# First retention outputs loaded and split during the last pair of gate columns of a streaming encoder layer

## The chip, the cores and the metric

One core of a Trainium2 chip. The metric is the device time of one execution in microseconds; the time before is the median of three runs. The profile is of one further execution. The engines: PE (TensorE, matmuls), DVE (VectorE), ACT (ScalarE), POOL (GpSimd) and SP (SyncE, which here only issues DMAs). Each engine takes its instructions in the order in which the program holds them.

## The reference

One step of a hybrid encoder layer over 1024 prompt tokens and 64 sample tokens, width 1024, all in float32:

```
rq, rk, rv, rg, sq, sk, sv, ga, gb = split(rms_norm(x) @ w_in)
A = (rms_norm(retention(rq, rk, rv)) * silu(rg)) @ w_ret_out     # 4 heads of 256
B = sliding_window_attention(sq, sk, sv, bias, sinks) @ w_swa_out  # 16 heads of 64
x += (sigmoid(ga) * A + sigmoid(gb) * B) @ w_mix_out
x += cross_attention(rms_norm(x), memory)                        # 256 memory tokens
x += swiglu(rms_norm(x))
y = rms_norm(x)
```

The sliding window takes chunks of 64 queries against their own and the two earlier chunks (192 keys). States, keys, values and memory keys and values are outputs too.

## The kernel before

Activations lie transposed: 8 tiles of 128 features by 1088 tokens. Float32 precision is made from two float32r parts: an operand is **split** into a high part (a cast on ACT, L123) and a low part (a subtraction on DVE, L124), and each product is three matmuls (high x high, high x low, low x high). `load` (L117) and `store` (L120) issue DMAs from SP. Weights come as 128x1024 pieces into two staging buffers `raw` and are split into `wq` tiles.

**The projections** run as pairs of column blocks. A pair is seven block products of a Strassen-like scheme (`strassen`, L205 to L208), in the order of the operands B11, B21, T2, T1, T3, B22, T4. Each product fills an accumulator of two PSUM banks (three such accumulators), which DVE adds up (L252, L563) and scales (L569); for gate columns ACT takes the sigmoid (L572) and issues the store (L658). The last pair of all is the last of `w_gb`.

**The places.** Two rings of eight SBUF places each hold the operands, two places an operand (ring 0: B11 in 4 and 5, T1 in 6 and 7, T4 in 0 and 1, the stage tiles for outputs in 2 and 3; ring 1: B21 in 0 and 1, T2 in 4 and 5, T3 in 6 and 7, B22 in 2 and 3). A later tile in a place waits until the last reader of the earlier one is through, so the places come free in the order of the products.

**The passage to attention** (`mix_phase`). Two streams of work are interleaved on PE. The sliding-window attention (`swa`) goes through 34 halves of chunks: scores `pss` (L934), softmax (DVE L944 or L947 with the bias, L949 to L954, ACT L956 and L958, DVE L959 and L960, POOL L962), transposes `pp` (L976), their copies `pT` (ACT L979, DVE L981), weighted values `pout` (L992). A `filler` puts other products between them: the last of the memory values (`pd<-wq,ms`), then the retention outputs times `w_ret_out` (`pd<-ret,wq`), with half an output block (12 matmuls) after each half chunk. `filler` first loads all retention outputs from the scratch tensor `d_gate[0]` in three groups of columns (384, 384, 320, eight loads each), through ten small tiles `lds`, and splits them into the eight `ret` tiles of ring 1; then come the weights, one unit `w_ret_out[m]` at a time.

**What sets the order.** A scheduler orders the instructions of each engine at build time; `tc.high_priority()` moves work up, `tc.issue_after(x)` places work behind instruction x in its order (it adds no wait on the chip). The order on PE of the passage is written out with `in_order`. The eight tiles `flat[0..7]` of ring 0 (places 4, 5, 6, 7, 0, 1, 2, 3) hold what attention reads: keys `kT` (flat[0], place 4, with three token tiles), queries `qTs` (flat[1] and flat[7]), bias (flat[2], place 6), token values `vT` (flat[5], place 1), transposed tokens `vts` (flat[4], place 0), and `lds` (flat[3] and flat[6], places 7 and 2).

Of the kernel before, what the change touches and what calls it, by code (L numbers as in the profile page):

```python
# [2 lines left out]

# [1 line left out]

# [14 lines left out]
P = 128  # L20
D = 1024
KT = D // P
# [3 lines left out]
CH = ((0, 384), (384, 384), (768, 320))  # L26
# [9 lines left out]
NPAIR = 8  # L36
NKEY = 192
KC = SEQ + P + SMP
# [71 lines left out]
class Kernel:  # L110
# [760 lines left out]
    def swa(self, ctx, fill):  # L871
        nc, tc, io = self.nc, self.tc, self.io
        if True:
# [2 lines left out]
            mm = nc.tensor.matmul  # L876

            flat = [t.rearrange("p a b -> p (a b)") for t in self.ring_tiles(0, KT, "swin", F32)]
            kT, vT = flat[0][:, :KC], flat[5][:, :KC]
            bias = flat[2][:, :NPAIR * NKEY].rearrange("p (a b) -> p a b", b=NKEY)  # L880
            sinks = self.sinks
            qTs = [t[:, :16 * 2 * 64].rearrange("p (i c e) -> p i c e", i=4, c=4) for t in (flat[1], flat[7])]
            vts = [flat[4][:, i * P:(i + 1) * P] for i in range(17)] + [flat[0][:, KC + i * P:KC + (i + 1) * P] for i in range(3)]
            self.lds = [t[:, i * 384:(i + 1) * 384] for t in (flat[3], flat[6]) for i in range(5)]
            with tc.high_priority():
                def tokens(dst, i, cache):
                    self.load(dst[:, :SEQ], self.d_skv[i, :, :SEQ])
                    self.load(dst[:, SEQ:SEQ + P], io[cache])
                    self.load(dst[:, SEQ + P:], self.d_skv[i, :, SEQ:])
# [5 lines left out]
            with tc.high_priority(), tc.issue_after(self.loaded):  # L895
                for e in range(2):
                    src = self.d_rb.rearrange("(p e) c -> e c p", e=2)[e, 63:63 + 64 * 255, :]
                    src = src.rearrange("(i c) p -> i p c", c=255)[:, :, :NKEY]
                    self.load(bias[e * 64:(e + 1) * 64], src)
            def keep():  # L900
                for src, o in ((kT, "o_sk"), (vT, "o_sv")):
                    self.store(io[o][0], src[:, SEQ - P:SEQ])
                    self.store(io[o][1], src[:, SEQ + SMP:KC])
# [21 lines left out]

            def scores(c, hf):
                ks, j0, nk = keys(c)
                if hf == 0 and c % 4 == 0 and c + 4 < 17:
                    self.load_queries(qTs, c + 4)
                qT = qTs[c // 4 % 2]  # L930
                pss = pw.tile([P, 2, 512], F32, tag="s", name="pss")
                for i in range(2):
                    for v in range(2):
                        self.last_mm = mm(pss[:, v, i * NKEY:i * NKEY + nk], qT[rows[v], 2 * hf + i, c % 4, :],  # L934
                                          kT[rows[v], ks:ks + nk], start=True, stop=True).ins
                quad = lambda x: x.rearrange("p (v h i) -> p v h i", v=2, h=2)[:, :, hf, :]
                snk = quad(sinks)
                t = sw.tile([P, 2, 2, NKEY], F32, tag="t", name="t")
                ps = pss[:, :, :2 * NKEY].rearrange("p v (i n) -> p v i n", n=NKEY)
                bs = bias.rearrange("p (v h i) n -> p v h i n", v=2, h=2)  # L940
                nm = sw.tile([P, 2, 2], F32, tag="nm", name="nm")
                if nk == NKEY:
                    fl = lambda x: x.rearrange("p v i n -> p v (i n)")
                    nc.vector.scalar_tensor_tensor(fl(t), pss[:, :, :2 * NKEY], 0.125, fl(bs[:, :, hf]), ALU.mult, ALU.add)  # L944
                else:
                    for v in range(2):
                        nc.vector.scalar_tensor_tensor(t[:, v, :, :nk], ps[:, v, :, :nk], 0.125, bs[:, v, hf, :, j0:],  # L947
                                                       ALU.mult, ALU.add)
                nc.vector.tensor_reduce(nm, t[:, :, :, :nk], AX.X, ALU.max)  # L949
                nc.vector.tensor_tensor(out=nm, in0=nm, in1=snk, op=ALU.max)  # L950
                nc.vector.tensor_scalar(nm, nm, -1.0, None, ALU.mult)
                den = sw.tile([P, 2, 2], F32, tag="den", name="den")
                es = sw.tile([P, 2, 2], F32, tag="es", name="es")
                nc.vector.tensor_tensor(out=es, in0=snk, in1=nm, op=ALU.add)  # L954
                for v, i in units:
                    nc.scalar.activation(t[:, v, i, :nk], t[:, v, i, :nk], AF.Exp, bias=nm[:, v, i:i + 1],  # L956
                                         accum_out=den[:, v, i:i + 1])
                nc.scalar.activation(es, es, AF.Exp)  # L958
                nc.vector.tensor_tensor(out=den, in0=den, in1=es, op=ALU.add)  # L959
                nc.vector.reciprocal(den, den)  # L960
                p = lambda x: x.rearrange("p v i n -> p (v i) n")
                nc.gpsimd.tensor_tensor(out=p(t)[:, :, :nk], in0=p(t)[:, :, :nk], op=ALU.mult,  # L962
                                        in1=den.rearrange("p v i -> p (v i)").unsqueeze(2).broadcast_to([P, 4, nk]))
                live[c, hf] = t
# [41 lines left out]
            n = len(halves)  # L1006
            for i in range(-2, n):
                if i > 0:
                    self.in_order(lambda: weigh(*halves[i - 1]))
                if i + 2 < n:  # L1010
                    self.in_order(lambda: scores(*halves[i + 2]))
                if i >= 0:
                    self.in_order(lambda: turn(*halves[i]))
                for pieces in next(fill):
                    self.in_order(lambda: next(pieces, None))
                if i == -2:
                    with tc.high_priority(), tc.issue_after(self.operand_loaded):
                        tokens(vT, 1, "cvT")
                if i == 8:
                    with tc.issue_after(self.loaded):  # L1020
                        keep()
# [23 lines left out]
    def filler(self):  # L1045

        nc, tc, io = self.nc, self.tc, self.io
        if True:
            def ld():
                self.lds.append(self.lds.pop(0))  # L1050
                return self.lds[-1]

            rets = self.ring_tiles(1, KT, "ret")

            def operands(c0, n):
                after = self.loaded
                for k in range(KT):
                    a = ld()
                    with tc.issue_after(after):
                        ins = self.load(a[:, :n], self.d_gate[0][k, :, c0:c0 + n])  # L1060
                    if c0 == 0:
                        self.operand_loaded = ins
                    self.split(a[:, :n], rets[k][:, 0, c0:c0 + n], rets[k][:, 1, c0:c0 + n])

            for c0, n in CH:
                operands(c0, n)
            us, h = self.first_units, H - 1
            for t in range(2):
                ps = self.dense_psum()
                for k in range(KT):  # L1070
                    x = self.ms[k][:, :, t * P:(t + 1) * P]
                    self.mm3(ps[:, :256], x[:, 0], x[:, 1], *us[k // 4][k % 4], k == 0, k == KT - 1)
                    if k == 3:
                        yield
                o = ld()[:, :256]
                with tc.high_priority():
                    nc.scalar.mul(o, ps[:, :256], self.mtok[:, t:t + 1])
                self.store(self.d_mv[h, :, t, :], o)
                self.store(io["o_mv"][t * P:(t + 1) * P, h * 256:(h + 1) * 256], o)
                yield  # L1080
            for m in range(KT):
                u = self.unit(io["w_ret_out"][m], KT)
                for c0, n in CH:
                    g = ld()
                    self.load(g[:, :n], self.d_gate[1][m, :, c0:c0 + n])
                    for ps in self.pieces(u, rets, c0, n):
                        if ps is None:
                            yield
                    nc.vector.tensor_tensor(out=g[:, :n], in0=ps, in1=g[:, :n], op=ALU.mult)
                    self.store(self.d_mix[m, :, c0:c0 + n], g[:, :n])  # L1090
                    yield
# [588 lines left out]
```

## Time and profile before

| | |
|---|---|
| median of 3 runs | 2251.56 us (2247.32 to 2252.81) |
| the profiled execution | 2246.01 us |
| its span, first to last instruction | 2244.2 us |
| mean granted clock of TensorE | 0.988 |
| last pair of gate columns, first matmul | 793.1 us after the span's start |
| first scores of the attention | 814.1 us |
| first product with retention outputs | 835.1 us |
| last scores of the attention | 1002 us |

Rows of a timeline give the start in us from the span's start, the duration, the engine, the line of the kernel, the operation with output <- input tiles, the size, and in brackets the idle time of the engine before it and what ended it. A row with xN has N instructions merged. Rows of a table of stretches give the length, the busy time of PE, PEld (weight loads), DVE, ACT and POOL with their instructions, the granted clock of TensorE, the busy share of the DMA engines and GB/s. DMA rows give the size of one transfer and the median time from issue to landing.

### The profile page before, as it was taken

How to read it: one execution, taken by the hardware profiler on the slowest of the kernel's cores; microseconds unless marked ns; L12 is line 12 of the kernel's file. 1: busy time of each engine (PE TensorE's matmuls, PEld its weight loads, DVE VectorE, ACT ScalarE, POOL GpSimd, SP SyncE). 2: the span in 40 equal slices, each digit the busy share in tenths (PEclk: the TensorE clock that was granted, in tenths of full speed). 3: DMA queues.
4: the chain of work that ended last, by engine and by line, in shares of the span. 5: the costliest groups of instructions: out<-in, count | busy, mean ns of one | idle time of the engine just before them, and what ended most of it. 6: DMA issues, size and time to landing. Idle time of an engine off the chain costs nothing.

```text
span 2244.2 us, 41644 instructions
## 1 busy us (share of the span) xinstructions
PE 2161.9 (96%) x16374; PEld 2097.0 (93%) x16374; DVE 1602.8 (71%) x2655; ACT 883.9 (39%) x1896; POOL 689.8 (31%) x466
## 2 busy tenths in 40 slices
PE   7899999999999989999999999999999999999996
PEld 6899999999999977779999998999999999999986
DVE  8995878676687568875455565676777777778587
ACT  7333333435444355553233343333222222344343
POOL 1441533342263112220000000015555556434462
PEclk9999999999999989999999999999999999999998
DMA  5433345443545475327343112422342332476233
GB/s 198 161 116 110 111 130 134 130 127 115 172 141 188 144 242 166 111 68 219 118 153 119 38 49 71 133 78 88 122 138 92 102 128 83 151 263 196 75 96 108
DMA packets 182598, 290.84 MB, mean 130 GB/s; under 512 B 40290, under 2 KB 110850, under 8 KB 182402
## 3 DMA queue, kind: packets, MB, share of 16 engines
q1 hardware_dynamic: 177794, 279.26, 39.2%
q10 hardware_dynamic: 4608, 8.91, 1.1%
q8 instruction: 129, 2.11, 0.4%
q14 instruction: 67, 0.55, 0.1%
HBM read 196.95 MB, written 91.16 MB: 128 GB/s over the span
## 4 chain that ended last, share of the span: by engine, by line
PE 80%; DVE 10%; DMA 4%; issue 2%; ACT 2%; POOL 1%; SPq 0%; DVEq 0%; ACTq 0%; POOLq 0%
PE pq L208 15%; PE pq L205 15%; PE pq L206 15%; PE pd L149 8%; PE pd L151 8%; PE pd L150 8%; DVE wq L124 2%; PE pout L992 1%; DMA hl<-d_op 1%; PE pp L976 1%; PE pss L934 1%; DVE T L124 1%; DVE B L124 1%; DMA qs<-d_qkv 1%; PE pk L691 1%
## 5 line engine op out<-in xcount | busy, mean ns | idle before, releaser
L124 DVE TENSOR_TENSOR wq<-raw,wq 128x512 fp32r<-128x512 f32 (+1 forms) x505 | 456.6, 908 | 126.4 <-ACT wq L123 124.2
L123 ACT CAST wq<-raw 128x512 fp32r<-128x512 f32 (+1 forms) x505 | 307.7, 614 | 562.6 <-PE pq L208 266.5
L205 PE MATMUL pq<-T,wq 128*128 128x272 f32 x1832 | 492.5, 289 | 5.6 <-DVE u L252 3.7
L206 PE MATMUL pq<-T,wq 128*128 128x272 f32 x1832 | 492.8, 289 | 0.0
L206 PE MATMUL pq<-B,wq 128*128 128x272 f32 x1592 | 430.1, 290 | 9.7 <-DVE B L124 9.5
L205 PE MATMUL pq<-B,wq 128*128 128x272 f32 x1592 | 428.0, 289 | 11.8 <-ACT wq L123 10.6
L208 PE MATMUL pq<-T,wq 128*128 128x272 f32 x1832 | 384.1, 290 | 3.6 <-DVE wq L124 3.6
L183 POOL TENSOR_TENSOR raw<-raw 128x512 f32<-128x512 f32 (+1 forms) x59 | 82.7, 1402 | 905.9 <-DVE wq L124 623.6
L205 PEld LDWEIGHTS pq<-T,wq 128*128 128x128 f32 x1832 | 346.0, 189 | 6.3 <-DVE u L252 3.7
L206 PEld LDWEIGHTS pq<-T,wq 128*128 128x128 f32 x1832 | 346.0, 189 | 0.3 <-issue 0.3
L208 PE MATMUL pq<-B,wq 128*128 128x272 f32 x1592 | 334.2, 290 | 0.0
L206 PEld LDWEIGHTS pq<-B,wq 128*128 128x128 f32 x1592 | 301.2, 189 | 12.2 <-DVE B L124 11.8
L205 PEld LDWEIGHTS pq<-B,wq 128*128 128x128 f32 x1592 | 300.8, 189 | 12.5 <-ACT wq L123 10.6
L208 PEld LDWEIGHTS pq<-T,wq 128*128 128x128 f32 x1832 | 291.0, 190 | 5.1 <-DVE wq L124 4.4
L208 PEld LDWEIGHTS pq<-B,wq 128*128 128x128 f32 x1592 | 253.5, 190 | 0.5 <-issue 0.3
L252 DVE TENSOR_TENSOR u<-pq,u 128x544 f32<-128x544 f32 x177 | 127.5, 721 | 112.3 <-PE pq L208 111.7
L186 POOL TENSOR_TENSOR raw<-raw 128x512 f32<-128x512 f32 (+1 forms) x59 | 83.1, 1408 | 133.8 <-DVE wq L124 126.2
L563 DVE TENSOR_TENSOR stage<-pq,u 128x544 f32<-128x544 f32 x112 | 80.3, 717 | 27.7 <-PE pq L208 25.3
L962 POOL TENSOR_TENSOR t<-t,den 128x768 f32<-128x768 f32 (+2 forms) x34 | 47.9, 1407 | 167.4 <-DVE nm L950 58.7
L184 POOL TENSOR_TENSOR raw<-raw 128x512 f32<-128x512 f32 (+1 forms) x59 | 88.1, 1494 | 3.7
L189 POOL TENSOR_TENSOR raw<-raw 128x512 f32<-128x512 f32 (+1 forms) x59 | 84.0, 1424 | 4.4
L1438 POOL TENSOR_TENSOR y<-u,y 128x544 f32<-128x544 f32 x38 | 61.9, 1638 | 76.3 <-DVE y L1436 52.0
(370 smaller groups left out, 4647.2 us busy)
## 6 DMA issues: line engine op xcount, KB each, us to landing
hl<-d_op SPq DMA_DIRECT2D x85, 272.0 KB, 4.0
d_qkv<-stage SPq DMA_DIRECT2D x44, 272.0 KB, 2.1
d_op<-stage SPq DMA_DIRECT2D x44, 272.0 KB, 2.1
d_op<-ht SPq DMA_DIRECT2D x44, 272.0 KB, 3.2
raw<-w_gate SPq DMA_DIRECT2D x22, 512.0 KB, 3.4
raw<-w_up SPq DMA_DIRECT2D x22, 512.0 KB, 3.6
d_gate<-stage ACTq DMA_DIRECT2D x32, 272.0 KB, 2.3
raw<-w_down SPq DMA_DIRECT2D x16, 512.0 KB, 4.4
```

What stands on the lines that cost most here:

```text
L123: self.last_cast = self.nc.scalar.copy(hi, src).ins
L124: return self.nc.vector.tensor_tensor(out=lo, in0=src, in1=hi.bitcast(F32), op=ALU.subtract).ins
L149: mm(ps, wh, xh, start=start, stop=False)
L150: mm(ps, wh, xl, start=False, stop=False)
L151: self.last_mm = mm(ps, wl, xh, start=False, stop=stop).ins
L184: tt(out=a21, in0=a21, in1=a22, op=add)
L186: tt(out=a11, in0=a22, in1=a11, op=sub)
L189: tt(out=a12, in0=a12, in1=a11, op=sub)
L205: mm(ps[:, c, :HC], w[:, 0, ks], x[:, 0, cs], start=start, stop=False)
L206: mm(ps[:, c, :HC], w[:, 0, ks], x[:, 1, cs], start=False, stop=False)
L208: self.last_mm = mm(ps[:, c, :HC], w[:, 1, ks], x[:, 0, c * HC:(c + 1) * HC], start=False, stop=stop).ins
L252: add = lambda out, a, b: nc.vector.tensor_tensor(out=out, in0=a, in1=b, op=ALU.add)
```

## The change

The eight `ret` tiles get their places of ring 1 in the order in which the last pair frees them (0, 1, 4, 5, 6, 7, 2, 3). The loads and splits of the first 384 columns are free to be scheduled from the moment when the first places come free; they go through five `lds` tiles in B11's first place (flat[0]), the other five (flat[5], T4's second place) join afterwards. The attention's tiles move: keys and the three token tiles to flat[2], bias to flat[3] (T1's places), values to flat[4] (T4's first place), transposed tokens to flat[6] (a stage place); the queries stay. `w_ret_out[0]` is loaded and split ahead of the other two groups of columns, which come behind the bias's load in the order; the load of the value tokens comes behind the bias too. The second load of queries (chunks 4 to 7), issued before with the first scores, comes behind the last load of retention outputs.

```diff
-            kT, vT = flat[0][:, :KC], flat[5][:, :KC]
-            bias = flat[2][:, :NPAIR * NKEY].rearrange("p (a b) -> p a b", b=NKEY)
+            kT, vT = flat[2][:, :KC], flat[4][:, :KC]
+            bias = flat[3][:, :NPAIR * NKEY].rearrange("p (a b) -> p a b", b=NKEY)
...
-            vts = [flat[4][:, i * P:(i + 1) * P] for i in range(17)] + [flat[0][:, KC + i * P:KC + (i + 1) * P] for i in range(3)]
-            self.lds = [t[:, i * 384:(i + 1) * 384] for t in (flat[3], flat[6]) for i in range(5)]
+            vts = [flat[6][:, i * P:(i + 1) * P] for i in range(17)] + [flat[2][:, KC + i * P:KC + (i + 1) * P] for i in range(3)]
+            self.lds, self.more_lds = ([t[:, i * 384:(i + 1) * 384] for i in range(5)] for t in (flat[0], flat[5]))
...
-                    self.load(bias[e * 64:(e + 1) * 64], src)
+                    self.bias_loaded = self.load(bias[e * 64:(e + 1) * 64], src)
...
-                if hf == 0 and c % 4 == 0 and c + 4 < 17:
+                if hf == 0 and c % 4 == 0 and 0 < c < 13:
                     self.load_queries(qTs, c + 4)
...
                 if i == -2:
-                    with tc.high_priority(), tc.issue_after(self.operand_loaded):
+                    with tc.high_priority(), tc.issue_after(self.bias_loaded):
                         tokens(vT, 1, "cvT")
+                    with tc.issue_after(self.last_operand):
+                        self.load_queries(qTs, 4)
...
-            rets = self.ring_tiles(1, KT, "ret")
+            rets = [self.rings[1].tile(f"ret{k}", slot=i) for k, i in enumerate((0, 1, 4, 5, 6, 7, 2, 3))]
 
             def operands(c0, n):
-                after = self.loaded
+                after = self.bias_loaded
                 for k in range(KT):
                     a = ld()
-                    with tc.issue_after(after):
-                        ins = self.load(a[:, :n], self.d_gate[0][k, :, c0:c0 + n])
-                    if c0 == 0:
-                        self.operand_loaded = ins
+                    with tc.issue_after(after) if c0 else nullcontext():
+                        self.last_operand = self.load(a[:, :n], self.d_gate[0][k, :, c0:c0 + n])
                     self.split(a[:, :n], rets[k][:, 0, c0:c0 + n], rets[k][:, 1, c0:c0 + n])
-
-            for c0, n in CH:
+                if c0 == 0:
+                    self.lds += self.more_lds
+
+            operands(*CH[0])
+            first = self.unit(io["w_ret_out"][0], KT)
+            for c0, n in CH[1:]:
                 operands(c0, n)
...
-                u = self.unit(io["w_ret_out"][m], KT)
+                u = self.unit(io["w_ret_out"][m], KT) if m else first
```

More of the change, by code (lines that the diff above doesn't have):

```diff
@@ L1 @@
 import math
-from contextlib import ExitStack, contextmanager
+from contextlib import ExitStack, contextmanager, nullcontext
 import numpy as np
```

## The prediction

> **What bounds the kernel now.** I read the engine shares and the chain of work on the page first, then the stretch where the change acts: where TensorE waits between 790 and 860 us, and what each queue does there.
>
> ```profile
> PE 2161.9 (96%) x16374; PEld 2097.0 (93%) x16374; DVE 1602.8 (71%) x2655; ACT 883.9 (39%) x1896; POOL 689.8 (31%) x466
> PE 80%; DVE 10%; DMA 4%; issue 2%; ACT 2%; POOL 1%; SPq 0%; DVEq 0%; ACTq 0%; POOLq 0%
> ```
>
> TensorE (PE) bounds the whole: 2161.9 of 2244.2 us. Only its 82 us of idle time, and matmuls at a low clock, can be won. The waits of PE from 790 to 1010 us (total, times, longest):
>
> ```profile
> PE pd L149 <- ACT wq L123: 7.9, 2, 5.2
> PE pp L976 <- POOL t L962: 1.2, 2, 0.8
> PE pout L992 <- ACT pT L979: 1.2, 1, 1.2
> ```
>
> Nearly all of it is the passage from the gate columns to the sliding-window attention (SWA). PE's timeline there (start, us, idle before and releaser in brackets):
>
> ```profile
> 817.55 0.58 PE L149 MATMUL pd<-wq,ms 128*128 128x256 f32 x1 [2.78 <-ACT wq L123]
> 823.31 0.28 PE L149 MATMUL pd<-wq,ms 128*128 128x256 f32 x1
> 826.24 0.66 PE L934 MATMUL pss<-swin,swin 64*128 64x64 f32 x8
> 829.65 0.33 PE L911 MATMUL pd<-ident,swin 128*128 128x128 f32 x1 [0.80 <-DMA swin<-d_skv]
> 835.14 0.69 PE L149 MATMUL pd<-ret,wq 128*128 128x384 f32 x1 [5.16 <-ACT wq L123]
> 841.50 0.63 PE L976 MATMUL pp<-ident,t 128*64 128x128 f32 x4
> 841.88 0.42 PE L149 MATMUL pd<-ret,wq 128*128 128x384 f32 x1
> 845.57 0.66 PE L976 MATMUL pp<-ident,t 128*128 128x128 f32 x4
> 845.98 0.42 PE L149 MATMUL pd<-ret,wq 128*128 128x384 f32 x1
> 849.52 0.65 PE L992 MATMUL pout<-pT,swin 128*64 128x256 f32 x4 [1.21 <-ACT pT L979]
> 851.88 0.66 PE L976 MATMUL pp<-ident,t 128*128 128x128 f32 x4 [0.85 <-POOL t L962]
> 856.15 1.04 PE L976 MATMUL pp<-ident,t 128*128 128x128 f32 x8
> ```
>
> There are two holes, 2.78 us before the last memory-value product and 5.16 us before the first retention output product, and after each the clock is low:
>
> ```profile
> 815.00:820.00 5.00, 2.31 (x9) 2.02 (x10) 3.17 (x6) 3.78 (x8) 0.00 (x0) 0.64 0.71 240
> 830.00:835.00 5.00, 0.00 (x0) 0.00 (x0) 3.50 (x12) 5.00 (x21) 1.71 (x2) 0.51 0.91 320
> 835.00:840.00 5.00, 4.24 (x12) 3.56 (x12) 5.00 (x10) 3.75 (x10) 0.23 (x1) 0.50 0.97 310
> ```
>
> (Busy time of PE, PEld, DVE, ACT, POOL, then granted clock, DMA share, GB/s.) After the first hole the slow pace lasts from 817.55 to 823.31, 5.8 us. After the second, the same three steps (12 matmuls, pout, scores) take 835.14 to 841.50, 6.36 us with 0.62 of waiting in it, and 841.88 to 845.57, 3.69 us, one step later: the low clock costs 5.74 - 3.69 = 2.05 us. Both holes end with a cast of ACT:
>
> ```profile
> 815.73 0.66 ACT L572 ACTIVATE stage<-stage 128x544 f32<-128x544 f32 x1 [2.33 <-DVE stage L569]
> 816.88 2.18 ACT L123 CAST wq<-raw 128x512 fp32r<-128x512 f32 x4 [0.49 <-ACT stage L572]
> 834.48 2.18 ACT L123 CAST wq<-raw 128x512 fp32r<-128x512 f32 x4
> ```
>
> **The change part by part.** The built program holds the same instructions: 24 loads and 24 splits of retention outputs (a cast on ACT, a subtraction on DVE), the same matmuls. What changes is where they stand.
>
> *Splits of the first 384 columns* (8 of 24) stand inside the last pair. Row durations of all splits:
>
> ```profile
> 838.45 2.40 DVE L124 TENSOR_TENSOR ret<-swin,ret 128x384 fp32r<-128x384 f32 x5
> 841.07 1.70 DVE L124 TENSOR_TENSOR ret<-swin,ret 128x320 fp32r<-128x320 f32 x4 [0.23 <-ACT ret L123]
> 836.55 1.70 ACT L123 CAST ret<-swin 128x384 fp32r<-128x384 f32 x4
> 794.79 0.32 SPq L117 DMA_DIRECT2D swin<-d_skv  x1
> 793.10 0.29 PE L205 MATMUL pq<-B,wq 128*128 128x272 f32 x1
> 814.11 0.66 PE L934 MATMUL pss<-swin,swin 64*128 64x64 f32 x8
> 794.00:814.00 20.00, 20.00 (x163) 19.96 (x161) 9.38 (x13) 4.88 (x8) 1.94 (x2) 1.00 0.78 227
> ```
>
> One costs 0.48 us of DVE (0.43 for 320 columns) and 0.43 of ACT. Eight add 3.8 to DVE's 9.38 and 3.4 to ACT's 4.88 of 20 us, beside a PE that is busy throughout. The pair's seven products run from 793.10 to 814.11, 3.0 us each; half through the first, at 794.79, the first place came free for a load. Each split waits for the product that frees its place (B21, T2, T3, B22, in this order), as the add standing next to it does, and three accumulators lie between an add and the product that needs its bank: I cost this at 0. Were the cover gone, the dearest place is one 0.5 us subtraction ahead of an add. The lower bound is 0 too.
>
> *The first hole stays.* ACT casts the w_mv pieces behind the last sigmoid (815.73), which hangs on the last product. Their loads now stand behind eight gate loads (192 KB each), the queries (1 MB) and the keys (0.6 MB) on SP. With their own 1 MB that is 4.2 MB; at the 227 GB/s of the last row it takes 18.5 us from 794.8, to 813, and the cast comes at 816.88. 0 us.
>
> *w_ret_out ahead of the other columns; values' load moved up.* The value tokens load when T4's first place is free (half through the last product, 812.6), so the 0.80 at 829.65 goes. The w_ret_out load waits for a staging buffer, freed by the second w_mv subtraction:
>
> ```profile
> 817.52 2.50 DVE L124 TENSOR_TENSOR wq<-raw,wq 128x512 fp32r<-128x512 f32 x4 [1.82 <-ACT wq L123]
> 829.62 0.81 SPq L117 DMA_DIRECT2D raw<-w_ret_out  x2
> raw<-w_ret_out SPq DMA_DIRECT2D x5, 512.0 KB, 5.9
> ```
>
> That is 818.8 instead of 829.62; SP holds six loads of the second 384 columns, all of the last 320, and two more units behind it. With the median of 5.9 us it lands at 824.7, its cast ends by 826, before PE needs it. So the first product of retention outputs no longer waits 5.16 and 0.62: PE gets there at 829.0 (826.24, two score steps, token transpose, pp), does its 12 matmuls at full pace and comes to the next pp at 832.3.
>
> *What is late next.* That pp (841.50 before) transposes the second softmax tile. Before, it was long ready:
>
> ```profile
> 830.83 0.61 POOL L962 TENSOR_TENSOR t<-t,den 128x256 f32<-128x256 f32 x1 [5.19 <-DVE nm L951]
> 829.54 0.68 DVE L949 TENSOR_REDUCE nm<-t 128x4 f32<-128x512 f32 x1
> 842.69 0.75 DVE L947 SCALAR_TENSOR_TENSOR t<-pss,swin 128x256 f32<-128x256 f32 x2
> ```
>
> In the changed order DVE has, between this tile's scores (which PE gives at 826.9) and its reciprocal (L960, on which POOL's scaling waits): 5 subtractions of 384 columns (2.4), 8 of 320 (3.4), 4 of w_ret_out (2.5), three score evacuations L947 (0.5, 0.75, 0.75), three maxima L949 (0.4, 0.7, 0.7), and about twelve small ones of 0.09 (1.1): 13.2 us. ACT likewise has the tile's last exponential behind the last cast. DVE is through at 840.1, POOL's 0.61 ends at 840.8, and PE stands from 832.3 to 840.8, 8.5 us. **The wait changes its place**: pp starts at 840.8 instead of 841.50.
>
> *After it*, the low clock comes again: pp 0.4, three steps in 5.74 (as after 835.14), pp 0.4, then four steps as from 841.88 to 845.98 (3.7): the next pp at about 851.0 (before 851.88), the one after, 4.27 later, at 855.2 (before 856.15). The 1.21 and 0.85 of waiting are gone, paid for by the slow steps that now come later. POOL scales the next two tiles right behind the first (by some 844, an estimate from the same rows), before PE asks for them. From 860 on PE waited for SWA only once,
>
> ```profile
> PE pp L976 <- POOL t L962: 0.4, 1, 0.4
> ```
>
> so nothing gives it back, and nothing more is won.
>
> **Sum:** 856.15 to 855.2, -1.0 us. On the profiled execution (2246.0, span 2244.2 and 1.8 around it) that is 2245.0; this execution lies 5.6 below the median 2251.56, so I put 2250.6 for the median.
>
> The Trainium skill, "TensorE: Matmul & The Clock Gate", Part 1, says that the gate closes after an idle window of about 3.4 us and that sustained work opens it again after about 3.4 us. The trace differs: the pace fell after only 2.78 us of idle and stayed low for 5.8 us. With the page's 3.4 us the steps after 840.8 would be done some 0.7 us sooner, an estimate from that page, and the sum -1.7.
>
> **The rivals.**
>
> *The holes go for good.* If DVE's list is through by 832, PE never stands: pp at 832.3 instead of 841.50 (-9.2), and the 1.21 and 0.85 go as well: about -10, 2241.5. For it: the cause of the longest wait is truly removed. Against: DVE's 13.2 us would have to fit in 5.4, and its order is fixed in the program; it decides only if those rows take less than half.
>
> *The transfers bind, and it gets slower.* From 818.8 until the last of the 24 loads, SP brings 3 x 512, 6 x 192, 8 x 160 and 4 x 64 KB: 4.3 MB, behind a load that waits for DVE.
>
> ```profile
> 819.00:847.00 28.00, 20.74 (x129) 17.61 (x128) 22.94 (x59) 20.41 (x64) 2.72 (x3) 0.74 0.93 305
> 805.00:810.00 5.00, 5.00 (x42) 5.00 (x41) 2.45 (x4) 0.00 (x0) 0.00 (x0) 1.00 1.00 206
> d_qkv<-stage SPq DMA_DIRECT2D x44, 272.0 KB, 2.1
> ```
>
> At 305 GB/s, with 2 us from issue to landing, they are in by 835, some 4 us before DVE wants the last; at the 206 of the other stretch, by 842: pp at 844 (+2.5), and the gate columns and units behind it late by as much again: +5, 2256. Below some 250 GB/s this decides. Against it: the bytes before 819 are fewer than those that moved at 305.
>
> *It does not do what it says*: the early loads come too late to split under the last pair. They are issued from 794.8, when B11's first place is free; at 227 GB/s the first five with the 1 MB of queries take 9 us, and the fifth place frees at 807: no.
>
> **How the numbers follow.** Wait moved: 0.65, from -4 to +2.5 (3 us of ACT and DVE order either way, and the executions before lay at 2247.3 to 2252.8). Holes gone: 0.15. Transfers bind: 0.15, half of it beyond 0.3%. None of these: 0.05. 0.3% is 6.8 us, about what a measurement of this kernel tells from no change. Faster 0.17, same 0.72, slower 0.11. The range leaves out the holes-gone case: 2243 to 2256.
>
> **What would show it.** Right: no wait before the first pd<-ret; a hole of 7 to 9 us before the second pp, released by POOL; 2.78 us before pd<-wq,ms unchanged; low clock near 845. Wrong: POOL's second scaling before 835, or PE waiting for a load of the gate columns, or for an add inside the last pair.

## The result, and the profile after

The changed kernel takes **2257.97 us** (median of 7 runs, 2257.38 to 2261.46), the kernel before on the same chip 2250.23 (7 runs, 2246.79 to 2255.4): ratio **1.0041**, 95% interval 1.0031 to 1.005. It is slower, by 7.7 us in the medians and 9 by the ratio, and above my range (2243 to 2256).

The shares of the page (busy time, then the chain that ended last) look as before:

```profile
PE 2167.4 (96%) x16374; PEld 2104.4 (93%) x16374; DVE 1602.7 (71%) x2655; ACT 885.4 (39%) x1896; POOL 687.2 (30%) x466
...
PE 81%; DVE 10%; DMA 4%; issue 2%; ACT 2%; POOL 1%; SPq 0%; DVEq 0%; ACTq 0%; POOLq 0%
```

The waits of PE tell more. This is the changed kernel from 780 to 1080 us (total, times, longest), a stretch that also takes in what follows the attention, the merge:

```profile
PE pd L149 <- DVE swa L124: 6.3, 1, 6.3
PE pp L976 <- POOL t L962: 6.0, 2, 5.6
PE pss L934 <- DVE t L947: 3.5, 1, 3.5
PE pd L149 <- ACT wq L123: 2.7, 1, 2.7
PE pd L150 <- DVE wq L124: 0.3, 1, 0.3
```

Lines two to five are the passage, where the change was made: 12.5 us of waiting. In the kernel before it is 12.4, the three lines in the prediction (7.9, 1.2, 1.2) and three smaller ones:

```profile
PE pd L911 <- DMA swin<-d_skv: 0.8, 1, 0.8
PE pss L934 <- DVE t L947: 0.7, 1, 0.7
PE pd L151 <- DVE wq L124: 0.6, 1, 0.6
```

So in the passage PE waits as long as before, in other places. The first line of the changed kernel is new, and stands 190 us behind it.

To see where the time went I split both profiled executions at five instructions of PE's timeline: the first matmul of the last gate pair, the first scores, the last scores, the first product of the merge (`pd<-swa`), and the first product with `w_mix_out` (`pd<-mix`), which follows the merge.

| us | before | changed | difference |
|---|---|---|---|
| start of span to last gate pair | 793.10 | 796.95 | +3.85 |
| last pair to first scores | 21.01 | 21.01 | 0 |
| first to last scores (the passage lies at its head) | 187.68 | 187.99 | +0.31 |
| last scores to first merge product | 32.32 | 38.82 | **+6.50** |
| first merge product to first product with `w_mix_out` | 96.00 | 98.82 | **+2.82** |
| from there to the end | 1114.09 | 1112.61 | -1.48 |
| span | 2244.2 | 2256.2 | +12.0 |

The first 3.85 us lie ahead of anything that was changed and are scatter: in the fourteen profiled executions of this study that pair starts between 793.1 and 797.1, and an experiment below whose instructions are those of the kernel before up to the merge starts it at 796.20. The last stretch scatters as well, from 1112.5 to 1118.8 us in the same fourteen. In the passage the two kernels differ by 0.31. The loss is at the merge: 6.50 and 2.82, 9.3 us together.

PE's timeline of the changed kernel there, with the last product of the filler and the first of the merge:

```profile
1038.12 0.31 PE L151 MATMUL pd<-ret,wq 128*128 128x320 f32 x1
1044.77 1.33 PE L149 MATMUL pd<-swa,wq 128*128 128x384 f32 x3 [6.34 <-DVE swa L124]
1045.90 0.52 PE L150 MATMUL pd<-swa,wq 128*128 128x384 f32 x1
...
1050.38 0.52 PE L149 MATMUL pd<-swa,wq 128*128 128x384 f32 x1
...
1051.13 0.34 PE L149 MATMUL pd<-swa,wq 128*128 128x384 f32 x1
```

And the same stretches of the two kernels (length, busy time of PE, PEld, DVE, ACT, POOL with instructions, granted clock, DMA share, GB/s), first before, then changed:

```profile
1035.00:1040.00 5.00, 5.00 (x30) 5.00 (x30) 4.39 (x9) 3.08 (x7) 0.00 (x0) 1.00 0.88 285
1040.00:1045.00 5.00, 5.00 (x30) 5.00 (x29) 2.02 (x5) 2.33 (x6) 0.00 (x0) 1.00 0.96 324
1045.00:1050.00 5.00, 5.00 (x30) 5.00 (x29) 4.74 (x10) 1.48 (x4) 0.00 (x0) 1.00 0.88 295
```

```profile
1040.00:1045.00 5.00, 0.23 (x1) 0.23 (x2) 2.97 (x7) 3.19 (x7) 0.00 (x0) 0.56 0.92 305
1045.00:1050.00 5.00, 5.00 (x16) 5.00 (x17) 3.46 (x8) 2.71 (x7) 0.00 (x0) 0.50 0.94 294
1050.00:1055.00 5.00, 5.00 (x27) 5.00 (x27) 1.67 (x3) 0.51 (x1) 0.00 (x0) 0.92 0.46 146
```

The reader should look at the counts, not the busy time: in the first 5 us after the hole PE is "busy" throughout and gets through 16 matmuls instead of 30. The hole costs 6.34, the low clock behind it some 2.8 (17 matmuls take 5.61 from 1044.77 to 1050.38, 0.33 each, and three more 0.75; in the kernel before one follows the other after 0.177), which is the 2.82 of the table.

**The mechanism.** The merge multiplies eight tiles `swa0` to `swa7` with `w_swa_out`; each sum runs over them in this order. They are the next tenants of ring 0 (places 4, 5, 6, 7, 0, 1, 2, 3) after the attention's tiles. The change moved the `lds` tiles, which the filler uses to its last store, from places 7 and 2 to places 4 and 1. So the place that comes free last, behind the filler's last two stores `d_mix`, was that of `swa6` before and is that of `swa0` now. In the kernel before the builder put the products of `swa0` to `swa5` for two sums, and of `swa0` to `swa4` for a third, ahead of the first with `swa6`: 51 matmuls, 9.0 us of cover at 0.177 each. With `swa0` missing no sum can start. SP's queue of the changed kernel shows the last store, and ACT's what follows it:

```profile
1040.54 0.32 SPq L120 DMA_DIRECT2D d_mix<-swin  x1
```

```profile
1042.48 0.51 ACT L123 CAST swa<-ld 128x384 fp32r<-128x384 f32 x1 [0.46 <-DMA ld<-d_swa]
1043.34 2.16 ACT L123 CAST swa<-ld 128x320 fp32r<-128x320 f32 x5 [0.35 <-DMA ld<-d_swa]
```

In the program the two casts of `swa0` that PE needs are the third and fourth of those five, with 384 columns each (the merged row hides that). The store issued at 1040.54 takes 3.6 us to land, the third cast starts at 1044.21, and PE goes on at 1044.77.

### The profile page after: what moved, and what is told of

The parts are those of the page before. It is cut to its first block, busy times and chain, and to the rows that moved or that the text cites. A ratio compares the mean times of both kernels' runs of the same rounds, so it can differ in the third digit from the quotient of the medians.

```text
span 2256.2 us, 41636 instructions
## 1 busy us (share of the span) xinstructions
PE 2167.4 (96%) x16374; PEld 2104.4 (93%) x16374; DVE 1602.7 (71%) x2655; ACT 885.4 (39%) x1896; POOL 687.2 (30%) x466
## 4 chain that ended last, share of the span: by engine, by line
PE 81%; DVE 10%; DMA 4%; issue 2%; ACT 2%; POOL 1%; SPq 0%; DVEq 0%; ACTq 0%; POOLq 0%
PE pq L208 15%; PE pq L206 15%; PE pq L205 15%; PE pd L149 8%; PE pd L151 7%; PE pd L150 7%; DVE wq L124 2%; PE pout L992 2%; PE pp L976 1%; DMA hl<-d_op 1%; PE pss L934 1%; DVE B L124 1%; DVE T L124 1%; PE pk L691 1%; DVE stage L563 1%
```

## The experiments

Three groups of four kernels (m1, b1, m3, m4; m2, m7, m5, m6; s1 to s4); those of a group ran on one chip with runs of the kernel before (medians there 2250.74, 2249.93 and 2248.98). Across groups only the ratios compare. Times are medians, ratios are to the kernel before. Beside them stand the two lengths of the table above from each profiled execution, which the scatter at the start doesn't touch. They repeat well: two pairs of kernels have the same passage (before and b1, changed and m1), and agree within 0.21 us.

| | us | ratio, 95% interval | first to last scores | to first merge product |
|---|---|---|---|---|
| before | 2250.23 | | 187.68 | 32.32 |
| changed | 2257.97 | 1.0041 (1.0031 to 1.005) | 187.99 | 38.82 |
| b1 | 2258.97 | 1.0042 (1.0029 to 1.0055) | 187.47 | 39.24 |
| m1 | 2250.83 | 1.0005 (0.9996 to 1.0014) | 187.90 | 32.32 |
| m3 | 2252.22 | 1.0003 (0.9992 to 1.0014) | 189.38 | 32.21 |
| m4 | 2249.53 | 0.9997 (0.9988 to 1.0006) | 185.20 | 32.21 |
| m2 | 2247.39 | 0.9995 (0.9986 to 1.0003) | 185.42 | 32.21 |
| m7 | 2251.05 | 1.0014 (1.0003 to 1.0024) | 189.85 | 32.21 |
| m5 | 2251.15 | 1.0010 (0.9998 to 1.0022) | 186.78 | 32.21 |
| m6 | 2248.34 | 1.0000 (0.9989 to 1.0011) | 185.27 | 32.32 |
| s1 | 2247.12 | 0.9988 (0.9976 to 0.9999) | 183.83 | 32.31 |
| s2 | 2246.23 | **0.9981** (0.9971 to 0.9991) | 183.04 | 32.21 |
| s3 | 2248.42 | 0.9995 (0.9983 to 1.0007) | 184.54 | 32.31 |
| s4 | 2248.51 | 0.9993 (0.9982 to 1.0004) | 185.23 | 32.31 |

A passage length is one execution, though, and part of it is chance. In all fourteen executions each stretch in which the granted clock is at 0.50 lasts 3.41 us or two, three or four times as long (but for the one that runs to the end of the program); so what a hole costs also depends on when it falls. Here are the stretches from the first to the second scores of s1 and of s2, with the same 58 matmuls and the same first hole of 2.18 us:

```profile
815.42:826.26 10.84, 8.32 (x58) 7.85 (x57) 7.86 (x18) 8.25 (x22) 1.59 (x3) 0.84 1.06 346
```

```profile
816.13:825.45 9.32, 6.80 (x58) 6.34 (x57) 6.07 (x15) 6.55 (x17) 1.28 (x3) 1.00 1.01 317
```

The clock fell in s1 and not in s2, which makes 1.5 us. A difference of that size between two passages is not shown by one execution of each.

**The merge: m1 and b1.** m1 mends it in the changed kernel (all eight places in another order), b1 spoils it in the kernel before (two places exchanged).

```diff
 m1, in merge_swa of the changed kernel
-            swas = self.ring_tiles(0, KT, "swa")
+            swas = [self.rings[0].tile(f"swa{k}", slot=i) for k, i in enumerate((5, 7, 3, 0, 6, 2, 1, 4))]
 b1, in merge_swa of the kernel before
-            swas = self.ring_tiles(0, KT, "swa")
+            swas = [self.rings[0].tile(f"swa{k}", slot=i) for k, i in enumerate((2, 5, 6, 7, 0, 1, 4, 3))]
```

> The changed kernel, with the eight swa tiles of the merge put into ring 0 in another order: the place whose last filler store comes last (place 4) takes swa7 instead of swa0, place 1 takes swa6. Theory A (the lost time is the wait of the first merge product for the operand that stands first in each sum and lies in the place that comes free last): the 6.3 us before the first pd<-swa go, and with them the low clock behind them, some 2.9 us (16 matmuls between 1045 and 1050 against 30 before, 27 against 30 in the next 5 us); 2258.0 - 9.2 = 2248.8 us, at or 1 to 2 us below the kernel before; PE shows no wait at pd<-swa over 1 us. Theory B (the loss is in the passage and in the start, the merge only shows it): 2256 to 2258, with a wait of 5 us or more at another product of the merge.

> The kernel before, with the places of swa0 and swa6 exchanged in the merge, so that swa0 lies in the place of the last filler stores (place 2); nothing else is changed. Theory A: the loss of the change appears with none of its parts in the passage: 6 us of waiting before the first pd<-swa, released by DVE's split of swa, and some 2.9 us at low clock; 2250.2 + 9 = 2259 us (ratio about 1.004). Theory B: no change, ratio 1.000, and no such wait.

Theory A holds in both directions. b1 has the changed kernel's time with the old passage; PE's wait and the first row of the merge in b1:

```profile
PE pd L149 <- ACT swa L123: 6.9, 1, 6.9
```

```profile
1043.91 1.33 PE L149 MATMUL pd<-swa,wq 128*128 128x384 f32 x3 [6.88 <-ACT swa L123]
```

In m1 PE waits for nothing from 1030 to 1080, and the stretches of its merge are full again:

```profile
1035.00:1040.00 5.00, 5.00 (x34) 5.00 (x33) 4.50 (x10) 4.38 (x9) 0.00 (x0) 1.00 0.96 324
1040.00:1045.00 5.00, 5.00 (x30) 5.00 (x29) 3.24 (x8) 2.66 (x6) 0.00 (x0) 1.00 0.90 287
```

The price is the one worked out above: 9 us expected of b1, 0.42% of 2250 (9.4) measured; in its profiled execution the merge takes 8.5 us longer than in the kernel before. m1, the change without this accident, is as fast as the kernel before. What is left is the question where the gain in the passage went; the other kernels stand on m1.

**The parts of the change: m2 and m7.** m2 puts w_ret_out[0] back behind the retention columns, m7 takes the early loads back.

```diff
 m2
-            first = self.unit(io["w_ret_out"][0], KT)
             for c0, n in CH[1:]:
                 operands(c0, n)
+            first = self.unit(io["w_ret_out"][0], KT)
 m7
-                    with tc.issue_after(after) if c0 else nullcontext():
+                    with tc.issue_after(after):
```

> As m1_merge_mended, but w_ret_out[0] is loaded and split behind all 24 groups of retention columns again, as in the kernel before. Theory A (the passage is paced by the sum of what DVE and ACT must do in it, not by which operand comes first): the wait of PE before the first pd<-ret comes back (3 us or more, from wq) and the waits before the second pp and the third scores shrink by about as much; within 2 us of m1, 2249 to 2253. Rival (each wait adds for itself): the forecast's 5.8 us of waiting come on top, 2255 us or more.

> As m1_merge_mended, but the first eight retention loads stand behind the bias again, so that no split is done under the last pair; places and the order of w_ret_out stay as changed. Theory A (paced by the list of DVE): eight subtractions of 0.48 us come back into the passage, PE waits 3 to 4 us longer in it than in m1, 2254 us. Rival (the early splits hide nothing, since the list waits for loads and not for work): within 1 us of m1.

m2 came out below both expectations: weights first, which I had counted as the source of the gain, **costs** 2.5 us of the passage (185.42 to 187.90) in these two executions; 1.9 of it are waits (10.5 against 12.4). The ratios go the same way, but their intervals overlap, and with the stores on POOL (s1 and s3 below) only 0.7 is left. The wait before the first `pd<-ret` comes back in m2 with 2.8 us, but the holes of 3.4 and 5.6 shrink to 1.6 and 1.0 (and ACT's copy pT makes a new one). PE's waits in m2 from 780 to 1080:

```profile
PE pd L149 <- ACT wq L123: 5.4, 2, 2.8
PE pout L992 <- ACT pT L979: 2.2, 1, 2.2
PE pss L934 <- DVE t L947: 1.6, 1, 1.6
PE pp L976 <- POOL t L962: 1.3, 2, 1.0
```

In m7 the early splits turn out to be worth 1.95 us (189.85 to 187.90), about half of the 3 to 4 that theory A gave them: eight subtractions are 3.8 us of DVE, but DVE also stands still in the passage, in m1 2.41 us for the cast of w_ret_out[0], which waits for its transfer.

**The order on DVE: m3, m4, m5.** m3 writes the other two groups of columns behind the memory values; m4 puts the value tokens behind w_ret_out[0]'s load; m5 is m4 with w_ret_out[0]'s splits behind the second tile's maximum (`self.scored` is its L949).

```diff
 m3, in filler
             first = self.unit(io["w_ret_out"][0], KT)
-            for c0, n in CH[1:]:
-                operands(c0, n)
...
                 yield
+            for c0, n in CH[1:]:
+                operands(c0, n)
             for m in range(KT):
 m4, in swa
-                    with tc.high_priority(), tc.issue_after(self.bias_loaded):
+                    with tc.high_priority(), tc.issue_after(self.loaded):
                         tokens(vT, 1, "cvT")
 m5, on m4
-            first = self.unit(io["w_ret_out"][0], KT)
+            raw0 = self.unit_raw(io["w_ret_out"][0], KT)
...
+                if m == 0:
+                    with tc.high_priority(), tc.issue_after(self.scored):
+                        u = self.unit_parts(raw0, KT)
...
```

> As m1_merge_mended, and the loads and splits of the second and third groups of columns are written behind the memory values, so that DVE has 3 instead of 16 of their subtractions between the reciprocals of the first and the second softmax tile. Theory A (the hole before the second pp hangs on the splits that DVE takes ahead of that tile's softmax): the waits of 5.6 us (pp from POOL) and 3.5 us (pss from DVE) shrink below 1.5 us each and the low clock after them goes; 6 to 9 us below m1, 2240 to 2243 us. Rival (the hole moves once more, to the first product with the second columns): a wait at pd<-ret of 4 us or more near 845 to 850, time within 2 us of m1.

> As m1_merge_mended, and the load of the value tokens stands behind the load of w_ret_out[0] on SP. Theory A (w_ret_out[0] came late because SP was held by the value tokens ahead of it, whose loads wait for the place and for earlier transfers): its load is issued 3 us sooner against the last pair (25.5 us after the pair's first matmul instead of 28.8), the 2.7 us before pd<-ret go, and with 7 instead of 16 splits ahead of the second reciprocal the hole before the second pp shrinks by 2 to 4 us; 3 us below m1. Rival (the value tokens then come too late for the token transposes): a wait of 1 us or more before them, released by the load, and no gain over m1.

> As m4_values_behind_weights, and DVE takes the subtractions of w_ret_out[0] behind the scores and the maximum of the second softmax tile instead of ahead of them. Theory A (paced by the list): the wait of 3.0 us before the third scores (from L947) goes below 0.7, the one before the second pp grows by 2 us or more; within 1.5 us of m4. Rival (the wait of PE's third scores is a stall of DVE behind a transfer, time in which DVE does nothing, and comes back as gain): 3 us below m4, 2246 to 2247.

In m3 the hole moved once more. POOL's second scaling comes 38.9 us after the pair's first matmul instead of 48.7, but 13 of the 16 subtractions now stand among the softmax steps of later tiles, and PE waits there, as its timeline shows (not at `pd<-ret`, which the rival named). The time is that of m1 (1.0003 against 1.0005), as the rival said:

```profile
842.12 0.65 PE L976 MATMUL pp<-ident,t 128*128 128x128 f32 x4 [0.38 <-POOL t L962]
...
848.83 1.09 PE L976 MATMUL pp<-ident,t 128*128 128x128 f32 x4 [1.03 <-POOL t L962]
...
858.41 1.33 PE L976 MATMUL pp<-ident,t 128*128 128x128 f32 x8 [3.57 <-POOL t L962]
```

m4 gained 2.7 us of the passage, but not by its mechanism: w_ret_out[0] is issued 28.28 us after the pair's first matmul, as in m1 (28.23), because SP stands just as long for the five loads now ahead of it. What changed is the order on DVE that the builder made of it, 7 subtractions instead of 16 ahead of the second reciprocal, and PE waits 9.2 us instead of 12.4. The ratio is 0.9997 against 1.0005, with overlapping intervals, less than the 3 us expected. (The 2.7 us that this expectation puts before `pd<-ret` are those before `pd<-wq,ms`; they stayed.) In m5 the waits went as theory A said: 3.04 us at the third scores become 0.68, and the second pp's 0.72 become 6.29 (the edit moves the later lines of the kernel down by two). The passage is 1.6 us longer than m4's:

```profile
830.04 0.72 PE L934 MATMUL pss<-swin,swin 64*128 64x128 f32 x8 [0.68 <-DVE t L947]
...
832.39 0.45 PE L149 MATMUL pd<-ret,wq 128*128 128x384 f32 x1 [0.94 <-ACT swin L913]
...
843.78 1.06 PE L978 MATMUL pp<-ident,t 128*64 128x128 f32 x4 [6.29 <-POOL t L964]
```

**Work off DVE: m6.** On m4, POOL does the subtractions of the last 320 columns.

```diff
+                    if c0 < 768:
+                        self.split(a[:, :n], hi, lo)
+                    else:
+                        nc.scalar.copy(hi, a[:, :n])
+                        nc.gpsimd.tensor_tensor(out=lo, in0=a[:, :n], in1=hi.bitcast(F32), op=ALU.subtract)
```

> As m4_values_behind_weights, and the eight subtractions of the last 320 columns are done by POOL, which is idle in the passage but for the scalings. Theory A (DVE's list sets the holes): eight times 0.43 us less on DVE, second tile's reciprocal behind 3 instead of 7 splits; PE's waits from 800 to 860 are 3 us less, 2246 to 2247 us. Rival (POOL takes each at 0.8 us or more, from the 0.61 of its 128x256 scaling, and they stand ahead of the scalings that pp waits for, or slow DVE beside them): pp waits for POOL 3 us or more longer, 2251 to 2254.

Neither: PE waits 3.7 us at the third scores, 2.2 at pp and 1.0 at pout, as long as in m4, and the passage is 185.27 against 185.20. So by itself DVE's work wasn't what bound here.

**SP's hold: s1 to s4.** The waits of SP's queue in the changed kernel from 800 to 830 us, and its rows there:

```profile
SPq L117 <- DMA d_gate<-stage: 10.0, 3, 5.7
```

```profile
816.56 0.34 SPq L117 DMA_DIRECT2D swin<-d_skv  x1
822.66 0.33 SPq L117 DMA_DIRECT2D swin<-cvT  x1
824.34 0.33 SPq L117 DMA_DIRECT2D swin<-d_skv  x1
824.76 0.85 SPq L117 DMA_DIRECT2D swin<-d_gate  x2
825.71 0.38 SPq L117 DMA_DIRECT2D raw<-w_ret_out  x1
```

SP waits for gate **stores** of ACT, with which the token values have nothing to do. In the built program every DMA, of SP's queue and of ACT's, takes the next of eight completion semaphores, and waits at its issue until the DMA that had it eight places earlier is complete. Three of SP's loads follow in this way on stores that hang on the last sigmoids and take long to land:

```profile
d_gate<-stage ACTq DMA_DIRECT2D x4, 272.0 KB, 7.0
```

The Trainium skill, "DMA: Bandwidth & Descriptors", "Anatomy of one DMA", says that a wait for a semaphore is kept by the issuing sequencer before dispatch; the rows above agree, since the loads behind the held one, issued at once when it is gone, are held as well. s1 (on m2), s3 (on m1) and s4 (on the kernel before) let POOL issue the four stores, whose DMAs take other semaphores; s2 is s1 with m6's subtractions.

```diff
-                    store = nc.scalar.dma_start if idx else self.store
+                    store = nc.gpsimd.dma_start if (idx, m) == (2, 6) else nc.scalar.dma_start if idx else self.store
```

> As m2_weights_back, and the four stores of the last pair's gate columns are issued by POOL instead of ACT. In the programs with ACT's stores each DMA takes one of eight completion semaphores in turn, and SP's loads of the token values wait for stores of ACT that had the same one (in the changed kernel they take some 7 us to land, SP stands from 816.9 to 822.7 and to 824.3). Theory A (this hold makes the retention loads and w_ret_out late): SP stands for the token values less than 2 us, w_ret_out[0] is issued some 5 us sooner after the pair's first matmul (32.3 us in m2), the 2.8 us before the first pd<-ret go; 2 to 4 us below m2, 2244 to 2246. Rival (DVE's list alone sets the holes): PE waits as long in sum as in m2 (10.5 us), 2247 to 2249.

> As s1_last_stores_by_pool, and POOL does the eight subtractions of the last 320 columns. Theory A (once the loads are in time, DVE's list is the next limit): 1 to 2 us below s1. Rival (as between m4 and m6, where it gave nothing, or POOL's queue with the stores ahead makes the scalings late): within 1 us of s1 or above it.

> As m1_merge_mended (the change with the merge mended, w_ret_out[0] ahead of the other columns), and the last pair's four gate stores are issued by POOL. Theory A (w_ret_out[0] and the columns came late because SP stood for ACT's stores): the 2.3 us that ACT stood for w_ret_out[0] go, PE's waits before the third scores and the second pp shrink by 3 us together; 2247 to 2248. Rival (16 splits and w_ret_out[0]'s four ahead of the second reciprocal are too many in any case): the hole before the second pp stays at 5 us or more, within 1 us of m1 (2250.8).

> The kernel before, and the last pair's four gate stores are issued by POOL. Theory A (the hold of SP by ACT's stores belonged to the kernel before as well: there SP needs 12.7 us for seven loads from 806.9): w_ret_out[0] is issued 3 us sooner or more, the 5.2 us before the first pd<-ret shrink by as much; 2246 to 2247. Rival (in the kernel before the loads wait for their lds tiles and not for stores): no change, 2249 to 2251.

In s1 the hold is gone (814.03, 814.41, 814.90), w_ret_out[0] is issued 2.8 us sooner, not 5 (29.47 after the pair's first matmul; SP then waits for `lds` tiles), and the wait before the first `pd<-ret` falls from 2.8 to 1.27. The stores still take 6.0 us to land (median of four); only no load of SP follows on them any more. The passage is 1.6 us shorter, less than the 2 to 4 expected. s2 takes another 0.8 of the passage, but this does not show that POOL's help counts: 1.5 us are the stretch compared above, ahead of POOL's first subtraction (829.07), and behind it s2 is 0.7 us longer than s1; the intervals of the two ratios overlap. So the rival of s2 stands. s2 has the lowest ratio, 0.2% under the kernel before, and its interval lies below 1. PE's timeline in s2, the holes that are left:

```profile
818.97 0.38 PE L149 MATMUL pd<-wq,ms 128*128 128x256 f32 x1 [2.18 <-ACT wq L123]
...
828.75 1.23 PE L934 MATMUL pss<-swin,swin 64*128 64x128 f32 x8 [2.64 <-DVE t L947]
...
833.18 0.69 PE L149 MATMUL pd<-ret,wq 128*128 128x384 f32 x1 [1.95 <-ACT wq L123]
...
847.09 0.92 PE L934 MATMUL pss<-swin,swin 64*128 64x192 f32 x8 [0.61 <-DVE t L944]
...
851.89 0.65 PE L992 MATMUL pout<-pT,swin 128*64 128x256 f32 x4 [1.21 <-ACT pT L979]
```

s3 is the change as I had reckoned it, with SP free: w_ret_out[0] is issued 25.15 us after the pair's first matmul (my forecast, 818.8, was 25.7), the third scores wait only 0.68, and the one long hole is the one I had forecast, 8.5 us before the second pp:

```profile
829.60 0.71 PE L934 MATMUL pss<-swin,swin 64*128 64x128 f32 x8 [0.68 <-DVE t L947]
...
842.36 1.06 PE L976 MATMUL pp<-ident,t 128*64 128x128 f32 x4 [7.85 <-POOL t L962]
```

Its passage is 3.4 us shorter than m1's all the same: 1.0 is less waiting (11.4 us against 12.4), and the rest is pace, since PE stands long in two places instead of three and the granted clock is low for 10.24 us of the passage instead of 17.07. So in one respect both expectations of s3 were right, in time the first, in the hole the rival. In s4 the load comes 7.9 us sooner (28.64 after the pair's first matmul, 36.52 before), the passage is 2.45 shorter, but the wait before `pd<-ret` stays at 4.93: ACT casts w_ret_out[0] at 834.89 right behind other work, where its place in ACT's order is. So there the order held the cast, and no longer the transfer; through which of the loads the 2.45 came I have not followed. The time (ratio 0.9993, interval up to 1.0004) is not told from no change. Between s4 and s3, the two kernels without the hold, the passage differs by 0.69 us in favour of the change.

## Why the prediction was wrong, point by point

- *The same instructions, splits under the last pair at 0 cost*: right. The pair takes 21.01 us in both, no wait of PE lies in it.
- *The first hole stays*: right, 2.7 before and after.
- *w_ret_out[0] loaded at 818.8*: too early. Counted from the pair it came 3.1 us later (28.76 against 25.7). I had named its staging buffer as the only thing it waits for; SP's hold for ACT's stores was missing, and s3 shows that nothing else was. It isn't special to the change: in the kernel before SP waits 11.6 us for the same stores, and s4's passage gains by the same edit.
- *No wait before the first `pd<-ret`*: right, but I had PE reach it without a stop. It stood 3.53 us before the third scores, since DVE's L947 of the second tile stands behind the subtractions of w_ret_out[0], which waited 2.4 us for the late transfer (ACT's cast, DVE's subtraction, then PE in the changed kernel):

```profile
830.54 1.14 ACT L123 CAST wq<-raw 128x512 fp32r<-128x512 f32 x2 [2.33 <-DMA raw<-w_ret_out]
```

```profile
831.19 1.29 DVE L124 TENSOR_TENSOR wq<-raw,wq 128x512 fp32r<-128x512 f32 x2 [2.39 <-ACT wq L123]
```

```profile
833.49 1.23 PE L934 MATMUL pss<-swin,swin 64*128 64x128 f32 x8 [3.53 <-DVE t L947]
...
835.63 0.67 PE L149 MATMUL pd<-ret,wq 128*128 128x384 f32 x1
...
846.46 1.06 PE L976 MATMUL pp<-ident,t 128*64 128x128 f32 x4 [5.63 <-POOL t L962]
```

  I had summed DVE's list as work; a list with a wait in it also moves the wait.
- *The wait changes its place*: right. A hole before the second pp, released by POOL; POOL's scaling came at 841.95 counted from the pair as before (forecast 840.2), and the hole is 5.63 instead of 8.5 because 3.53 had been waited already. Low clock from 845 to 850 (0.55 granted) as said.
- *-1.0 us*: the passage took +0.31, 1.3 us off. The two items above are the cause as far as s3 tells, where the load comes in time: its passage is 3.1 us shorter than that of the kernel before, and 0.7 shorter than s4's, which lacks the hold too. A small slip beside it: the three full-pace steps of 3.69 us end at 845.57, not 845.98; the sum uses 3.7 and stands.
- **From 860 on, nothing gives it back**: this is the step that failed. I looked at the waits of the kernel *before* behind 860, and there was one of 0.4. But the change moves tiles between places of ring 0, and I had priced the move only where the attention reads them. The next tenants of the places, eight tiles of the merge in a fixed order, were never costed: 6.34 us of waiting and 2.82 at low clock, which b1 brings without the rest of the change and m1 takes away.
- *The rivals*: none of them was it. That the time came near my "transfers bind" (2256) is chance, the mechanism is another: the gate columns arrived in time, and no wait of PE in the passage ends with them.

The Trainium skill, "TensorE: Matmul & The Clock Gate", Part 1, gives some 3.4 us of sustained work until the clock is full again. Behind the 2.69 us hole the trace agrees: the granted clock is 0.50 from 822.15 to 825.57, 3.4 us, and 1.00 on both sides. Behind the 6.34 us hole it differs, with 6.1 us from PE's first product to the full clock:

```profile
1044.77:1050.85 6.08, 6.08 (x19) 6.08 (x20) 3.69 (x8) 2.94 (x7) 0.00 (x0) 0.50 0.94 300
```

With the page's 3.4 the merge would have cost some 1.2 us less (2.7 us fewer at 0.32 instead of 0.177 a matmul), an estimate from that page; the measured rows decide.

What stays open: why weights first makes a worse order of the lists while SP is held (the builder chooses the order, by durations that it assumes), how much of each passage difference under 2 us is the chance of the clock, and the sum of the parts, which I measured each with the others in place.

## What to carry to other kernels

When tiles change places in a ring, follow each place to its next tenant, and ask which part of the next stage lands in the one that comes free last: an operand that stands first in every sum stops everything, the same wait for a later one is hidden. An engine's list is a sum of work and of the waits in it, so moving work ahead of a critical chain also moves the wait for its transfer there. And before ordering loads, look at what the queue itself waits for: here it was another engine's stores, through a shared set of completion semaphores.

## What the runs showed of the hardware that was not expected

- A stretch at granted clock 0.50 lasts 3.41 us or a whole multiple of it, up to 13.65, in all fourteen executions (the one that runs to the end of the program aside). After a hole of 6.34 or 6.88 us 6.1 us of it lie behind PE's next matmul, after one of 2.69 3.4; a hole of 2.18 brought 3.41 us in s1 and none in s2.
- POOL takes 0.86 us for a 128x320 subtraction (median of 8, in s2), DVE 0.48 (the same eight in the kernel before). The Trainium skill, "GPSIMD Engine Reference", "Engine selection", puts GPSIMD at about half the pace of VectorE for two operands; the trace comes near it.
- A store of 272 KB issued by ACT takes 7.0 us to land here, at a DMA share of 0.7 to 1.1 in the 5 us stretches around it (in the prediction's row, 2.1 us for stores of that size).
- With the same instructions up to there, the last gate pair starts anywhere between 793.1 and 797.1 us, and the stretch behind the merge takes 1112.5 to 1118.8: single profiles can't tell 4 us of a change. Stretches counted from an instruction near it can, up to the chance of the clock.
